# Long GpSimd operations in pieces of 256 columns, and three projections in the first token tile, in a two-layer hybrid decoder step

## The chip, the cores and the metric

The kernel runs on one core of a Trainium2 chip. Its engines have queues of their own: PE is TensorE (matrix products), DVE is VectorE (called Vector here), ACT is ScalarE, POOL is GpSimd (called Pool), SP issues DMAs. The metric is the time of one execution on the device in microseconds, the median of the runs.

## The reference

Two layers of a hybrid decoder over 1024 prompt tokens and 8 x 4 sampled tokens, 1056 in all, with a model width of 1024:

```python
def rms_norm(x, g):
    y = xf * lax.rsqrt(jnp.mean(xf * xf, axis=-1, keepdims=True) + EPS)
    return y * g
...
# each layer
#   x = x + W_out [ SWA-GQA-sink-attn(u) | Mamba2-SSD(u) ],  with u = RMSNorm(x)
#   x = x + SwiGLU(RMSNorm(x))
# W_in gives columns [q 512 | k 128 | v 128 | z 1024 | xBC 1536 | dt 16]
```

The columns xBC pass a causal convolution of four taps and a SiLU; they are 8 blocks of 128 columns of x (two heads of 64 each), two blocks of B and two of C. The SSD part scans 16 heads in chunks of 128 tokens with decays that come from dt; its output is gated by z and normed. The attention part has 8 query heads, 2 key heads, a window of 128 and a sink.

## The kernel before, in words

**Layout and products.** The activations lie with the model width on the partitions and the tokens along the columns. The tokens are cut into three token tiles of 352 columns (`TW`). Every projection is made in fp32r as three products of high and low halves: high x high (L293), high weight x low activation (L294), low weight x high activation (L295), over 8 blocks of 128 rows (k), so 24 products a token tile and 72 a block of 128 output columns. The projection `d` (dt, 16 columns) has two products a k (L289), 16 a tile. The low half of an activation (`alo`) is made by Vector or Pool (`split`, L248, and in the first norm L487) after ACT has made the high half (`ahi`).

**Weights.** `load_next` fetches the next weight by DMA on SP (L278), ACT makes its high half (L266), Pool its low half in one operation (L267). A weight is asked for one projection ahead (`AHEAD = 1`). Of the weights, 52 of W_in and 16 of the SSD rows of W_out have 8 k-blocks (1024 columns), 16 of the attention rows of W_out have 4 (512).

**Order.** The program is written once; a scheduler and the object `flow` decide the order on each engine. `proj(...)` makes one or several projections together, token tile by token tile, and calls `flow.tick()` after each tile and projection; side work pushed into `flow` (generators such as `steps`, `prep`, `both(j)`, which runs `ssd(j)`) goes a step on at a tick.

**The opening of a layer.** `d`, conv 10 (C of the first group, x10) and then conv 8 (B, x8) are projected. `steps` works out dt and the cumulated decays from `d`. Then come x0 to x7, z0 to z7 (the gates, L860, L864), v, q and k. In layer 0 a special piece of code makes the first norm from rows: squares on ACT (L473), transposes on PE (L467), products and casts by k.

**An SSD head pair (`ssd(j)`)**, twice for 512 tokens each: decays arrive by DMA in `bc`, ACT makes exponentials (L739, L740), Pool multiplies them by C (L741), Vector multiplies with the mask (L742); Vector's L732 makes x times dt or decay for PE's L748, which makes the states, and PE's L778 makes the outputs. Vector's L309 to L311 are the steps of a reciprocal root, L655 copies the convolution's three old columns, L1271 adds W_out's product to x.

## Time and profile before

| What | Value |
|---|---|
| Median of 3 runs | 2900.59 us (2896.8 to 2905.93) |
| The profiled execution's own time | 2900.49 us |
| Its span, first to last instruction | 2898.6 us |
| Mean granted clock of PE | 0.985 |
| PE busy | 2825.6 us (97%) |
| Vector busy | 1642.5 us (57%) |
| ACT busy | 1114.6 us (38%) |
| Pool busy | 983.5 us (34%) |

Busy times come from one profiled execution. A granted clock of 1.00 is 2.4 GHz, 0.5 is 1.2 GHz. The line numbers are those of the kernel before; an idle time in brackets on a row is that of the engine just before it, with the operation that ended it.

### The profile page before, as it was taken

How to read it: one execution, taken by the hardware profiler on the slowest of the kernel's cores; microseconds unless marked ns; L12 is line 12 of the kernel's file. 1: busy time of each engine (PE TensorE's matmuls, PEld its weight loads, DVE VectorE, ACT ScalarE, POOL GpSimd, SP SyncE). 2: the span in 40 equal slices, each digit the busy share in tenths (PEclk: the TensorE clock that was granted, in tenths of full speed). 3: DMA queues.
4: the chain of work that ended last, by engine and by line, in shares of the span. 5: the costliest groups of instructions: out<-in, count | busy, mean ns of one | idle time of the engine just before them, and what ended most of it. 6: DMA issues, size and time to landing. Idle time of an engine off the chain costs nothing. (4 is left out here: it accounts for less than half of the span.)

```text
span 2898.6 us, 46682 instructions
## 1 busy us (share of the span) xinstructions
PE 2825.6 (97%) x18456; PEld 2725.1 (94%) x18456; DVE 1642.5 (57%) x3639; ACT 1114.6 (38%) x2326; POOL 983.5 (34%) x884
## 2 busy tenths in 40 slices
PE   7999999999999999999988999999999999999999
PEld 6989898889999999999988898988899999999999
DVE  7765648756348862333487565587553678523232
ACT  5775737644212111111247666476431121112121
POOL 4343337435222222222243333365442222222221
PEclk8999999999999999999999999999999999999999
DMA  4222222102123321211222212220021333111112
GB/s 170 90 83 66 73 67 98 33 17 72 39 61 106 96 87 37 59 34 55 75 90 73 86 46 90 63 99 19 26 73 34 88 92 117 56 48 45 52 37 82
DMA packets 308323, 197.78 MB, mean 68 GB/s; under 512 B 28255, under 2 KB 287623, under 8 KB 308073
## 3 DMA queue, kind: packets, MB, share of 16 engines
q1 hardware_dynamic: 308072, 194.79, 22.4%
q8 instruction: 146, 2.39, 0.3%
q14 instruction: 73, 0.59, 0.1%
q10 hardware_dynamic: 32, 0.01, 0.0%
HBM read 171.49 MB, written 25.30 MB: 68 GB/s over the span
## 5 line engine op out<-in xcount | busy, mean ns | idle before, releaser
L293 PE MATMUL g<-ahi,whi 128*128 128x352 f32 x3744 | 1229.2, 329 | 6.6 <-DVE big L1271 5.8
L295 PE MATMUL g<-ahi,w 128*128 128x352 f32 x3744 | 1219.3, 326 | 0.0
L294 PE MATMUL g<-alo,whi 128*128 128x352 f32 x3744 | 1217.9, 325 | 0.0
L267 POOL TENSOR_TENSOR w<-w,whi 128x1024 fp32r<-128x1024 f32 (+2 forms) x248 | 512.4, 2066 | 1207.6 <-ACT whi L266 954.1
L293 PEld LDWEIGHTS g<-ahi,whi 128*128 128x128 f32 x3744 | 710.9, 190 | 21.5 <-issue 12.0
L294 PEld LDWEIGHTS g<-alo,whi 128*128 128x128 f32 x3744 | 713.5, 191 | 8.1 <-issue 4.1
L295 PEld LDWEIGHTS g<-ahi,w 128*128 128x128 f32 x3744 | 713.0, 190 | 4.8 <-issue 4.1
L266 ACT CAST whi<-w 128x1024 fp32r<-128x1024 f32 (+2 forms) x248 | 225.4, 909 | 663.6 <-PE g L294 636.3
L295 PE MATMUL g<-A,w 128*128 128x352 f32 x1104 | 357.2, 324 | 0.0
L293 PE MATMUL g<-A,whi 128*128 128x352 f32 x1104 | 356.8, 324 | 0.0
L294 PE MATMUL g<-F,whi 128*128 128x352 f32 x960 | 310.0, 323 | 0.0
L373 DVE TENSOR_TENSOR big<-g,big 128x352 f32<-128x352 f32 x240 | 125.4, 522 | 235.7 <-PE g L295 235.4
L295 PEld LDWEIGHTS g<-A,w 128*128 128x128 f32 x1104 | 208.1, 188 | 0.0
L293 PEld LDWEIGHTS g<-A,whi 128*128 128x128 f32 x1104 | 207.7, 188 | 0.0
L1350 DVE SCALAR_TENSOR_TENSOR F<-F,xdds 128x128 f32<-128x128 f32 x512 | 201.6, 419 | 9.6
L1335 DVE TENSOR_TENSOR R<-R,g 128x352 f32<-128x352 f32 x132 | 68.9, 522 | 218.4 <-PE g L295 217.1
L294 PEld LDWEIGHTS g<-F,whi 128*128 128x128 f32 x960 | 181.0, 189 | 0.0
L1332 ACT ACTIVATE R<-R 128x352 f32<-128x352 f32 x132 | 65.6, 497 | 297.3 <-DVE R L1331 297.0
L244 ACT CAST A<-R 128x352 fp32r<-128x352 f32 x132 | 64.1, 486 | 282.2 <-DVE R L1335 281.0
L669 DVE SCALAR_TENSOR_TENSOR big<-R,vc,big 128x352 f32<-128x352 f32 (+2 forms) x240 | 138.2, 605 | 21.8 <-ACT big L667 21.0
L741 POOL TENSOR_TENSOR F<-F,A 128x1024 f32<-128x1024 f32 x32 | 83.5, 2610 | 111.7 <-ACT F L740 111.7
L1331 DVE TENSOR_TENSOR R<-g,sc 128x352 f32<-128x352 f32 x88 | 45.9, 521 | 125.6 <-PE g L295 122.9
(366 smaller groups left out, 3529.4 us busy)
## 6 DMA issues: line engine op xcount, KB each, us to landing
w<-in_w_gate_up_dram SPq DMA_DIRECT2D x88, 512.0 KB
w<-in_w_in_dram SPq DMA_DIRECT2D x44, 512.0 KB
F<-acd SPq DMA_DIRECT2D x32, 512.0 KB
out_dram<-F SPq DMA_DIRECT2D x42, 256.0 KB
w<-in_w_down_dram SPq DMA_DIRECT2D x32, 320.0 KB
w<-in_w_down_dram SPq DMA_DIRECT2D x40, 256.0 KB
xd<-big SPq DMA_DIRECT2D x16, 528.0 KB
big<-xd SPq DMA_DIRECT2D x16, 528.0 KB
```

Source lines behind the costliest of these rows:

```text
L244: SC.copy(hi, src)
L266: SC.copy(hi, raw)
L267: G.tensor_tensor(lo, raw, hi.bitcast(F32), op=ALU.subtract)
L293: TE.matmul(out, lhsT=hi[:, k, c], rhs=xh, start=(start and k == 0), stop=False)
L294: TE.matmul(out, lhsT=hi[:, k, c], rhs=xl, start=False, stop=False)
L295: TE.matmul(out, lhsT=lo[:, k, c], rhs=xh, start=False, stop=(stop and k == nk - 1))
L373: flow.anchor = V.tensor_tensor(d, pt[:, 0:TW], d, op=ALU.add)
L669: flow.anchor = V.scalar_tensor_tensor(d, r(w), c_w(l, w, m), d, op0=ALU.mult, op1=ALU.add)
L741: G.tensor_tensor(bc, bc, ct[:, sl].unsqueeze(1).to_broadcast([P, 2, 512]), op=ALU.mult)
L1332: SC.activation(sg[t], sg[t], AF.Silu)
L1335: flow.anchor = V.tensor_tensor(sg[t], sg[t], pt[:, 0:TW], op=ALU.mult)
L1350: V.scalar_tensor_tensor(st[:, jj, :], bb[:, t, :], xdds[:, j, b * 4 + t:b * 4 + t + 1], st[:, jj, :], op0=ALU.mult, op1=ALU.add)
```

## The change

It has three parts. Pool's low halves of W_in and W_out weights are made in operations of two k-blocks (256 columns), those of gate, up and down as before. Pool's product of C and decays (128x1024) is made in four operations of 256 columns. And conv 8 is projected together with `d` and conv 10 in one `proj`, so that a token tile has 16 + 24 + 24 products, with `steps` pushed after it; the first norm of layer 0 becomes a plain loop over the token tiles, in which the squares of a tile stand ahead of its transposes, and Pool makes the low halves of six of the eight k in every tile (in tile 0 before: four).

```diff
--- before.py
+++ after.py
@@ -264,7 +264,10 @@
         hi = mk("whi", [P, nk, cw], F32R, bufs=3)
         lo = mk("w", [P, nk, cw], F32R, bufs=WB)
         SC.copy(hi, raw)
-        G.tensor_tensor(lo, raw, hi.bitcast(F32), op=ALU.subtract)
+
+        n = nk if k[1] in ("gu", "down") else 2
+        for a in range(0, nk, n):
+            G.tensor_tensor(lo[:, a:a + n], raw[:, a:a + n], hi[:, a:a + n].bitcast(F32), op=ALU.subtract)
         wready[k] = hi, lo
 
     def weights(key):
@@ -456,48 +459,29 @@
     u = act_tiles()
     rb = slot("F2", [P, T])
 
-    sizes = [[P if b < 8 else NS for b in range(3 * t, 3 * t + 3)] for t in range(NT)]
-
-    def blocks(t):
-        return slice(3 * t * P, 3 * t * P + sum(sizes[t]))
-
-    def rows_to_columns(t, src):
-        pt = pbank()
-        for i, m in enumerate(sizes[t]):
-            TE.transpose(pt[:, i * P:i * P + m], src(i)[0:m], ident[0:m, 0:m])
-        return pt[:, 0:sum(sizes[t])]
-
-    def roots(t):
-        for i, m in enumerate(sizes[t]):
+    for t in range(NT):
+        bs = range(3 * t, 3 * t + 3)
+        n = [P if b < 8 else NS for b in bs]
+        c0, w = 3 * t * P, sum(n)
+        for b, m in zip(bs, n):
             sq = slot("F1", [P, D])
-            SC.activation(sq[0:m], xr[3 * t + i][0:m], AF.Square, accum_out=s9[0:m, 3 * t + i:3 * t + i + 1])
-        return rsqrt("r3", s9[:, 3 * t:3 * t + 3], D, bufs=2)
-
-    def columns(t):
+            SC.activation(sq[0:m], xr[b][0:m], AF.Square, accum_out=s9[0:m, b:b + 1])
+
+        def rows_to_columns(src):
+            pt = pbank()
+            for i, m in enumerate(n):
+                TE.transpose(pt[:, i * P:i * P + m], src(i)[0:m], ident[0:m, 0:m])
+            return pt[:, 0:w]
+
         for k in range(KD):
-            pt = rows_to_columns(t, lambda i: xr[3 * t + i][:, k * P:(k + 1) * P])
-            (SC.copy if k % 2 and t else V.tensor_copy)(x[k][:, blocks(t)], pt)
-
-    def first_norm(t, y):
-        SC.copy(rb[:, blocks(t)], rows_to_columns(t, lambda i: y[:, i:i + 1].to_broadcast([P, P])))
+            pt = rows_to_columns(lambda i: xr[3 * t + i][:, k * P:(k + 1) * P])
+            (SC.copy if k % 2 and t else V.tensor_copy)(x[k][:, c0:c0 + w], pt)
+        y = rsqrt("r3", s9[:, 3 * t:3 * t + 3], D, bufs=1)
+        SC.copy(rb[:, c0:c0 + w], rows_to_columns(lambda i: y[:, i:i + 1].to_broadcast([P, P])))
         for k in range(KD):
             s = mk("nu", [P, TW], bufs=3)
             V.scalar_tensor_tensor(s, x[k][:, tsl(t)], g_mix(0, k), rb[:, tsl(t)], op0=ALU.mult, op1=ALU.mult)
-            hi = SC.copy(u[0][t][:, k, :], s)
-            (V if k % 4 == 3 or (k % 2 and t == 0) else G).tensor_tensor(u[1][t][:, k, :], s, u[0][t][:, k, :].bitcast(F32), op=ALU.subtract)
-        return hi
-
-    y = roots(0)
-    columns(0)
-    y1 = roots(1)
-    hi = first_norm(0, y)
-    columns(1)
-
-    with tc.issue_after(hi.ins):
-        y2 = roots(2)
-    first_norm(1, y1)
-    columns(2)
-    first_norm(2, y2)
+            split(u[0][t][:, k, :], u[1][t][:, k, :], s, V if k % 4 == 3 else G)
     vrow = slot("F1", [P, P])
     wrow = slot("F1", [P, P])
     SY.dma_start(out=cst[:, P:], in_=A["const"][:, P:])
@@ -738,7 +722,9 @@
                         SC.activation(tt[:, hh, c * P:(c + 1) * P], bc[:, hh, c * P:(c + 1) * P], AF.Relu, bias=acum[:, cc:cc + 1], scale=-1.0)
                 SC.activation(tt, tt, AF.Exp, scale=-1.0)
                 SC.activation(bc, bc, AF.Exp)
-                G.tensor_tensor(bc, bc, ct[:, sl].unsqueeze(1).to_broadcast([P, 2, 512]), op=ALU.mult)
+                for hh in range(2):
+                    for q in range(0, 512, 256):
+                        G.tensor_tensor(bc[:, hh, q:q + 256], bc[:, hh, q:q + 256], ct[:, hf * 512 + q:hf * 512 + q + 256], op=ALU.mult)
                 V.tensor_tensor(tt, tt, cm[:, hf * 4:hf * 4 + 4, :].rearrange("p c q -> p (c q)").unsqueeze(1).to_broadcast([P, 2, 512]), op=ALU.mult)
                 yield
             for hf in range(2):
@@ -896,9 +882,8 @@
         ct = slot("A0", [P, T])
         bt = mk("big", [P, T], bufs=8)
         proj(("d", 16, lambda t, pt: V.tensor_scalar(dtT[:, tsl(t)], pt[0:32, 0:TW], h16[:, l:l + 1], None, op0=ALU.add)),
-             conv(10, ct))
+             conv(10, ct), conv(8, bt))
         flow.push("steps", steps())
-        proj(conv(8, bt))
         flow.push("prep0", prep(0, ct, bt), 2)
         xs(0)
         xs(1)
```

**Where it moves instructions.** On PE, at the start of layer 1, in token tile 0, the products of `d` (`g_14184`) and of x10 (`g_14202`) alternated over the k before:

```order
L289 MATMUL g_14184<-alo_13572,whi_13808 16x352
L294 MATMUL g_14202<-alo_13572,whi_14174 128x352
L295 MATMUL g_14202<-ahi_13569,w_14175 128x352
L289 MATMUL g_14184<-ahi_13569,whi_13808 32x352
L293 MATMUL g_14202<-ahi_13569,whi_14174 128x352
L289 MATMUL g_14184<-alo_13572,whi_13808 16x352
L289 MATMUL g_14184<-ahi_13569,whi_13808 32x352
```

After it `g_14357` is `d`, `g_14375` is x10 and `g_14428` is x8 (lines L292, L296, L297, L298 are 289, 293, 294, 295 of before):

```order
L292 MATMUL g_14357<-alo_13730,whi_13966 16x352
L297 MATMUL g_14375<-alo_13730,whi_14332 128x352
L298 MATMUL g_14375<-ahi_13727,w_14333 128x352
L292 MATMUL g_14357<-ahi_13727,whi_13966 32x352
L296 MATMUL g_14375<-ahi_13727,whi_14332 128x352
L298 MATMUL g_14428<-ahi_13727,w_14342 128x352
L296 MATMUL g_14428<-ahi_13727,whi_14341 128x352
L297 MATMUL g_14428<-alo_13730,whi_14341 128x352
L298 MATMUL g_14428<-ahi_13727,w_14342 128x352
L296 MATMUL g_14428<-ahi_13727,whi_14341 128x352
L297 MATMUL g_14428<-alo_13730,whi_14341 128x352
L298 MATMUL g_14428<-ahi_13727,w_14342 128x352
```

Eleven products of x8 in a row (seven of them shown) now stand ahead of the next low product of `d`; in the kernel before all of x8 in this place came behind x10's tiles.

On Pool, at the start of layer 1, the low halves of the weights of x10 and x8 (`w_`) and of the first token tile's activations (`alo_`) stood so before:

```order
L267 TENSOR_TENSOR w_14175<-w_14172,whi_14174 128x1024
L248 TENSOR_TENSOR alo_13572<-nu_13976,ahi_13569 128x352
L248 TENSOR_TENSOR alo_13572<-nu_13980,ahi_13569 128x352
L248 TENSOR_TENSOR alo_13572<-nu_13984,ahi_13569 128x352
L267 TENSOR_TENSOR w_14181<-w_14178,whi_14180 128x1024
L248 TENSOR_TENSOR alo_13572<-nu_13992,ahi_13569 128x352
```

And after the change (L270 is the low half, now of 256 columns; `R_` is a convolution's buffer):

```order
L270 TENSOR_TENSOR w_14333<-w_14330,whi_14332 128x256 x4
L637 MEMSET R_14453 128x3
L248 TENSOR_TENSOR alo_13730<-nu_14134,ahi_13727 128x352
L248 TENSOR_TENSOR alo_13730<-nu_14138,ahi_13727 128x352
L248 TENSOR_TENSOR alo_13730<-nu_14142,ahi_13727 128x352
L270 TENSOR_TENSOR w_14342<-w_14339,whi_14341 128x256 x4
L248 TENSOR_TENSOR alo_13730<-nu_14150,ahi_13727 128x352
```

Each weight's row has become four operations, and the order between the weights and the activations' low halves stayed.

On ACT, at the start of layer 0, the squares (L473) of row blocks 6 to 8 (`F_22`, `F_23`) stood behind the casts of the first token tile (`ahi_117`) before:

```order
L486 CAST ahi_117<-nu_231 128x352
L486 CAST ahi_117<-nu_235 128x352
L486 CAST ahi_117<-nu_239 128x352
L473 ACTIVATE F_69_283,s_81<-F_22_111 128x1024
L473 ACTIVATE F_70_285,s_81<-F_23_113 128x1024
L473 ACTIVATE F_71_287,s_81<-F_24_115 32x1024
```

After it they are L468 (with `F_22`, `F_23`, `F_24`) and stand among copies of transposed rows (L478, L480) and the casts, which are now made by `split` (L244):

```order
L480 COPY F_31_126<-p_188 128x384
L468 ACTIVATE F_78_323,s_81<-F_22_114 128x1024
L478 COPY big_68<-p_236 128x384
L244 CAST ahi_120<-nu_193 128x352
L468 ACTIVATE F_79_325,s_81<-F_23_116 128x1024
L244 CAST ahi_120<-nu_197 128x352
L468 ACTIVATE F_80_327,s_81<-F_24_118 32x1024
```

The first of the three squares now stands ahead of the first cast, the second ahead of the second and the third behind it.

On PE, counted in products of projections, the four head pairs j = 0 to 3 of each layer stand 48 products later than before (the first L748 of layer 0 after 408 products instead of 360), j = 4 stands 24 later, and those from j = 5 where they stood.

## Rows read from the trace of the kernel before

**Rows 1.** Page, part 1: busy us, share of span, instructions of each engine.
```profile
PE 2825.6 (97%) x18456; PEld 2725.1 (94%) x18456; DVE 1642.5 (57%) x3639; ACT 1114.6 (38%) x2326; POOL 983.5 (34%) x884
```

**Rows 2.** Stretches: from, to, length, busy us of each engine, clock, DMA.
```profile
21.00:60.00 39.00, 32.70 (x149) 25.14 (x147) 32.83 (x69) 19.97 (x43) 17.44 (x18) 0.77 0.44 155
60.00:81.30 21.30, 21.30 (x133) 19.37 (x133) 14.28 (x31) 10.35 (x17) 9.66 (x12) 0.92 0.21 73
520.00:1450.00 930.00, 930.00 (x5802) 912.36 (x5801) 479.01 (x1013) 239.58 (x513) 279.51 (x252) 1.00 0.20 59
1459.20:1506.10 46.90, 39.90 (x241) 34.54 (x240) 38.75 (x86) 21.73 (x43) 27.28 (x24) 0.93 0.23 71
```

**Rows 3.** What PE waited for: total us, times, longest.
```profile
PE p L748 <- DVE F L732: 14.9, 6, 4.5
PE g L293 <- DVE big L1271: 5.8, 2, 2.9
```

**Rows 4.** Timeline, 211 to 216 us: start, duration, engine, line, operation, idle.
```profile
212.05 2.35 POOL L267 TENSOR_TENSOR w<-w,whi 128x1024 fp32r<-128x1024 f32 x1
...
212.26 2.48 DVE L864 TENSOR_TENSOR big<-big,nu 128x320 f32<-128x320 f32 x1 [2.41 <-ACT nu L860]
...
215.37 0.67 DVE L732 TENSOR_TENSOR F<-p,dt 128x512 f32<-128x512 f32 x1
...
215.50 0.71 PE L748 MATMUL p<-F,A 128*128 128x128 f32 x4 [4.46 <-DVE F L732]
```

**Rows 5.** Vector's instructions by line and shape: busy us, mean ns, idle.
```profile
L864 DVE TENSOR_TENSOR big<-big,nu 128x352 f32<-128x352 f32 x32 | 20.8, 655 | 51.1 <-ACT nu L860 51.1
```

**Rows 6.** Timeline of 494 to 503 us (Pool's operation in a row is x4).
```profile
494.47 4.01 POOL L248 TENSOR_TENSOR alo<-big,ahi 128x352 fp32r<-128x352 f32 x4
...
495.67 0.99 DVE L310 SCALAR_TENSOR_TENSOR F<-F 128x192 f32<-128x192 f32 x1
...
498.87 2.46 POOL L267 TENSOR_TENSOR w<-w,whi 128x1024 fp32r<-128x1024 f32 x1
...
499.17 2.38 DVE L310 SCALAR_TENSOR_TENSOR F<-F 128x192 f32<-128x192 f32 x1
...
501.47 0.51 DVE L1271 TENSOR_TENSOR big<-g,big 128x352 f32<-128x352 f32 x1
...
502.04 0.43 PE L293 MATMUL g<-ahi,whi 128*128 128x352 f32 x1 [2.91 <-DVE big L1271]
```

**Rows 7.** Timeline, 113 to 118 us.
```profile
113.96 2.44 POOL L741 TENSOR_TENSOR F<-F,A 128x1024 f32<-128x1024 f32 x1 [9.49 <-ACT F L740]
...
114.25 2.21 DVE L655 COPY R<-R 128x3 f32<-128x3 f32 x1
...
117.07 1.27 PE L748 MATMUL p<-F,A 128*128 128x128 f32 x5 [3.00 <-DVE F L732]
```

**Rows 8.** Timeline of Vector and PE: last low half, 192nd product.
```profile
65.21 0.53 DVE L487 TENSOR_TENSOR alo<-nu,ahi 128x352 fp32r<-128x352 f32 x1 [0.55 <-ACT ahi L486]
...
80.96 0.32 PE L295 MATMUL g<-ahi,w 128*128 128x352 f32 x1
```

**Rows 9.** Timeline of ACT: first of three squares, row blocks 6 to 8.
```profile
29.38 1.05 ACT L473 ACTIVATE F<-F 128x1024 f32<-128x1024 f32 x1
```

**Rows 10.** Timeline of Pool and PE, layer 1: last low halves, 192nd product.
```profile
1493.07 2.17 POOL L248 TENSOR_TENSOR alo<-nu,ahi 128x352 fp32r<-128x352 f32 x2 [1.47 <-ACT ahi L244]
...
1505.91 0.32 PE L295 MATMUL g<-ahi,w 128*128 128x352 f32 x1
```

**Rows 11.** Pool's instructions by line and shape: busy us, mean ns, idle.
```profile
L267 POOL TENSOR_TENSOR w<-w,whi 128x1024 fp32r<-128x1024 f32 x160 | 389.6, 2435 | 780.2 <-ACT whi L266 613.5 <-issue 165.0 <-POOL rc L665 0.8
...
L267 POOL TENSOR_TENSOR w<-w,whi 128x512 fp32r<-128x512 f32 x56 | 72.4, 1293 | 242.1 <-ACT whi L266 190.6 <-issue 51.5
```

**Rows 12.** Timeline of Pool and PE: C times decays, its reader.
```profile
176.08 6.38 POOL L741 TENSOR_TENSOR F<-F,A 128x1024 f32<-128x1024 f32 x2 [0.79 <-ACT F L740]
...
190.05 1.20 PE L778 MATMUL p<-F,A 128*64 128x128 f32 x18
```

## The prediction

> **What bounds the kernel now.** I read the page's list of busy times first. TensorE (PE) is busy 97% of the span [rows 1], so nothing is won by making another engine do less; only the time in which PE waits, or runs at its lower clock, can go. The reader should see 2898.6 - 2825.6 = 73 us of waiting in [rows 1], which is the whole stock together with the stretches at the lower clock. Next I cut the span into stretches. From 520 to 1450 us PE is busy 930.00 of 930.00 us at a granted clock of 1.00 [rows 2]: nothing to win there, and 930 / 5802 = 0.160 us is the price of one PE instruction at full clock. The start of layer 0 is the opposite: between 21 and 60 us PE does 149 instructions, which at 0.160 would be 23.8 us, in 39.0 us at a clock of 0.77; from 60 to 81.3 it is busy all the time. The start of layer 1, 1459.2 to 1506.1, is busy 39.90 of 46.90 us [rows 2].
>
> The list of waits then names what PE waited for [rows 3]. Hardly any of it names Pool: it names Vector operations. So I looked on the timeline at what held Vector. At 212 us Vector's product `big<-big,nu` (L864) lasts 2.48 us, beside a low half on Pool (L267, 2.35 us) that began 0.21 us earlier and ends 0.34 us before it; PE's L748 then waits 4.46 us for Vector's next operations, L732 [rows 4]. The same L864, one tenth wider, takes 655 ns on average elsewhere [rows 5], so it stood still for some 1.8 us of Pool's operation. At 499 us L310 takes 2.38 us beside a low half of 2.46 us, and PE waits 2.91 us for the L1271 behind it; the same operation took 0.99 us at 495.67, between short Pool operations [rows 6]. At 114 us a copy of three columns (L655) takes 2.21 us beside Pool's C times decays (L741, 2.44 us), and PE waits 3.00 us [rows 7]. These Vector operations read or write SBUF only; they and a running Pool operation exclude each other. L748 at 1645 us and L293 behind L1271 at 1932 us wait in the same way behind the same pairs of layer 1; the totals 14.9 and 5.8 us in [rows 3] contain them.
>
> **The change, part by part.** *1. Three products in the first token tile, and the rewritten first norm, layer 0.* The work stays the same: d, x10 and x8 are 16 + 24 + 24 products a tile. What moves is x8's 72. In the kernel before, 133 PE instructions are left to do after 60 us, at 0.160 each, and the last of the three groups' products begins at 80.96 us, although the last low half of the norm is done at 65.21 + 0.53 = 65.74 us [rows 8]. With x8 joined, the 48 products of its tiles 0 and 1 can go into the 39.0 - 23.8 = 15.2 us in which PE waited or ran slow: 48 x 0.160 = 7.7 us. With all 72 it is 11.5. I take the middle, -9.5. The bounds: -15 if that stretch were filled entirely; -3 if the three squares (1.05 us each, [rows 9]) that now stand between ACT's casts put the whole chain of the norm off by 3.15 us and the low clock stays, so that 48 products cost twice 0.160 while they fill waits (7.7 - 3.15, less a share for the clock). Pool also makes six instead of four of the first tile's eight low halves: two operations of 1.0 us (four L248, of the same size, in 4.01 us, [rows 6]) instead of two of 0.53 on Vector [rows 8], 0.9 us, inside these bounds. Nine small matmuls of `steps` go behind the 192 products; they keep their price.
>
> *2. The same in layer 1.* There 241 instructions x 0.160 = 38.6 us fill 46.9, so 8.3 us are free [rows 2]. The last low half lands at 1493.07 + 2.17 = 1495.24, and the last product begins 10.7 us later, at 1505.91 [rows 10]. The 48 products of x8's tiles 0 and 1 would be 7.7 us again, but they have only the idle 46.9 - 39.9 = 7.0 us to go into, and a part of it stands at the front, where nothing of x8 is ready either. I take -5, between 0 and -8.3.
>
> *3. Pieces.* The 68 input and ssm output weights of 1024 columns become four pieces, the 16 of 512 two, C times decays (32 times) four; gate, up and down stay. From the means 2435 ns for 1024 columns and 1293 for 512 [rows 11], a column costs 2.23 ns and an operation 0.15 us besides, so a piece takes 0.15 + 256 x 2.23 ns = 0.72 us and four take 2.89 instead of 2.44. A Vector operation that meets Pool then stands behind at most one piece, and keeps its turn if Vector gets in between two Pool operations. [Rows 6] show that it does: four Pool operations in a row take 4.01 us from 494.47, and L310 begins and ends within them. At each of the five places only one held Vector operation stands ahead of the ones PE needs (L864, L310, L655); L732 and L1271 behind them read PSUM and ran at 0.67 and 0.51 us. So each wait shrinks by 2.44 - 0.72 = 1.7 us: 5 x 1.7 = -8.5. The bounds: 0 if the pieces merely follow one another, and -20.7 if all of the waits 14.9 + 5.8 of [rows 3] vanish.
>
> *4. What the pieces cost.* Pool's own work grows by (68 + 32) x 0.45 + 16 x 0.15 = 47 us, spread over the two stretches that hold the attention and SSD parts. Pool is busy 34% [rows 1], and the list of PE's waits has none for L267 or L741; the cover is that a weight's low half is made one product ahead, 3 x 24 x 0.160 = 11.5 us, and that C times decays at 176.08 to 182.46 is read by PE only at 190.05 [rows 12], 7.6 us later. If that cover were gone, each weight would be 0.45 us late at least. Besides this, the heads' work of j = 0 to 3 comes later on PE (in layer 0 the first L748 after 408 products instead of 360, as the order has it), so that waits fall elsewhere. Bounds: 0 and +15 (three or four new waits like the 4.46); I take +3.5, less than one such wait, since the places themselves stay of one kind.
>
> **The sum.** -9.5 - 5 - 8.5 + 3.5 = -19.5 from the profiled execution's 2900.49 us gives **2881 us**. The median of the three runs shown is 2900.59, the same, so nothing is corrected. All bounds together would give 2900.49 - 44 = 2856 and 2900.49 + 12 = 2912 (-3, 0, 0, +15); they won't all fall on one side, so I use 2864 to 2900.
>
> **A rule that speaks against the pieces.** In [rows 4, 6, 7] the operation that began first, on Pool, ran at its usual speed and Vector's stood still. The Trainium skill, page "SBUF — State Buffer", section "Who interferes with whom", says that Vector and GpSimd share one pair of ports as an exclusive lock, which whoever issues first holds for the whole instruction while the other is blocked. By that rule a weight in four pieces has to win the lock four times, and a Vector operation may come in between each time; the page gives no price for it, and by it alone four pieces could take four Vector operations longer; rival D is this case, worked out from rows alone. The trace agrees with the rule as far as it holds Vector up; [rows 6] show both sides taking turns.
>
> **The rivals.**
> *A. Layer starts gain nothing.* The norm's own chain on ACT, Vector and Pool sets the end, and x8's products put PE's transposes off, which feed the chain. For it: Vector is busy 32.83 of 39.0 us there, as much as PE [rows 2]. Against it: after 65.74 us there was no norm left, and PE still had 15 us to do. It would give 2900.49 - 8.5 + 3.5 = 2895.5, within the 0.3% that a measurement of this kernel can tell from no change (8.7 us: 2891.9 to 2909.3).
>
> *B. Slower: the heads run into new waits.* With three products ahead of them, `steps` and the first four heads of each layer begin 48 products (7.7 us) later against the gates z that read them. Each head that comes too late costs a wait such as L748's 4.46 us [rows 4]. It decides when the new waits exceed the 19.5 + 3.5 = 23 us of gain, five such waits, and is slower by the measure at seven: eight, one a head in both layers, give 8 x 4.46 = 36 and 2900.49 - 23 + 36 = 2913. For it: PE's order changes there for about a thousand products of each layer. Against: the order of each head stays as it was, and heads from j = 5 stand where they stood.
>
> *C. Pieces don't let Vector in.* If four pieces run without a gap, Vector waits 2.89 us instead of 2.44 at each place: 5 x 0.45 = +2 instead of -8.5. Against it [rows 6]. It would give 2900.49 - 14.5 + 3.5 + 2 = 2891.5, on the edge of no change.
>
> *D. Pool starves.* If each piece waits for a Vector operation of 0.7 us (L864, [rows 5]), a low half takes 2.89 + 4 x 0.7 = 5.7 us. That is still under the 11.5 us of one projection, so PE waits only where two weights and C times decays come together. With the whole +15 of part 4 it would give 2900.49 - 23 + 15 = 2892.5, just within no change.
>
> **Chances.** The forecast and its neighbourhood below 2891.9: 0.66. A: 0.13; B: 0.08; C: 0.07, half of it on each side of the edge; D in a form that eats the gain: 0.06, most of it within 0.3%. Faster by over 0.3%: 0.66 + 0.04 + 0.02 = 0.72. Within: 0.13 + 0.03 + 0.02 = 0.18. Slower: 0.08 + 0.02 = 0.10. The range 2864 to 2900 leaves out B, a bad D, and a little of A and of the gains over 36 us: about 2 in 10.
>
> **What would show it.** Step 1 is right if the last of the 192 products of d, x10 and x8 ends near 71 us instead of 81.3, and step 2 if it ends near 1501 less what step 1 saved. Step 3 is right if Pool's pieces take about 0.72 us, L864 of 320 columns falls from 2.48 us to 1.4 or less (0.66 + 0.72), and the waits for L732 and L1271 at the five places are 1 to 3 us. The prediction is wrong if new waits of PE for L732, L742 or for the gates appear between 100 and 500 us or 1530 and 1930 us, or if PE's stretch from 21 to 60 us is as slow as before with the x8 products still behind it.

## The result and the profile after

The changed kernel takes 2866.4 us (median of four runs, 2858.3 to 2873.8) against 2903.26 before: a ratio of 0.9874, with a 95% interval of 0.984 to 0.9908, so 27 to 46 us less. A second measurement (below, with the experiments) gave 2859.83 against 2904.59, a ratio of 0.9842 (0.9829 to 0.9856). Both say faster. The forecast of 2881 was 15 to 21 us too high: the first median lies 2.4 us inside its range of 2864 to 2900, the second 4.2 us below it.

The profiled execution took 42.1 us less than that of before (span 2856.5 against 2898.6). The page's head and its list of busy times:

```profile
span 2856.5 us, 47073 instructions
...
PE 2809.2 (98%) x18456; PEld 2710.3 (95%) x18456; DVE 1623.0 (57%) x3637; ACT 1097.8 (38%) x2314; POOL 1050.1 (37%) x1202
```

PE's idle time, span less busy, is 2856.5 - 2809.2 = 47.3 us; it was 73.0 [rows 1]. So 25.7 us come from waits that are gone, and 16.4 from matmuls that ran faster, since their number is the same (x18456): more of them at the higher clock (the mean granted clock is 0.993, against 0.985).

The first stretches of [rows 2] at the same times, and 520 to 1400 us, since layer 1 begins earlier now (from, to, length, then busy time and instructions of PE, weight loads, Vector, ACT and Pool, then the granted clock):

```profile
21.00:60.00 39.00, 36.38 (x217) 29.10 (x216) 38.55 (x79) 22.12 (x47) 24.12 (x28) 0.96 0.46 156
60.00:81.30 21.30, 21.30 (x133) 20.97 (x132) 16.22 (x46) 12.25 (x23) 9.97 (x18) 0.92 0.30 98
520.00:1400.00 880.00, 880.00 (x5488) 864.02 (x5487) 446.60 (x939) 220.23 (x463) 268.12 (x248) 1.00 0.20 58
```

Between 21 and 60 us PE now does 217 instructions instead of 149, at a clock of 0.96 instead of 0.77. From 520 to 1400 us it is busy without a gap, as before.

The list of PE's waits:

```profile
PE p L823 <- ACT sc L819: 7.6, 4, 2.8
...
PE g L296 <- DVE big L1256: 5.8, 2, 2.9
```

The wait of L748 for L732, 14.9 us in six times in [rows 3], has no row any more (its lines are now L734 and L716). The wait behind the output projection's sum, L1271 then and L1256 now, is 5.8 us as it was. In front stands one that grew, for a copy of ACT's (L819, L833 before) in the work on the sampled tokens' states: 7.6 us, where it was 2.7.

The last of the 192 products of d, x10 and x8, in layer 0 and in layer 1, on PE's timeline of the changed kernel (both answer to [rows 8] and [rows 10]):

```profile
65.87 0.32 PE L298 MATMUL g<-ahi,w 128*128 128x352 f32 x1
```

```profile
1479.99 0.32 PE L298 MATMUL g<-ahi,w 128*128 128x352 f32 x1
```

In layer 0 it begins at 65.87 us instead of 80.96, 15.1 us earlier. In layer 1 the first of the 192 begins at 1437.65 (1459.28 before), so the stretch takes 42.3 us instead of 46.6.

Pool's and Vector's groups by line and shape (busy us, mean ns of one), and last Vector's L864 of 320 columns in the kernel before:

```profile
L270 POOL TENSOR_TENSOR w<-w,whi 128x256 fp32r<-128x256 f32 x304 | 237.6, 811 | 261.4 <-ACT whi L266 169.7 <-issue 90.0 <-POOL rc L649 0.8
L270 POOL TENSOR_TENSOR w<-w,whi 128x1024 fp32r<-128x1024 f32 x92 | 221.2, 2404 | 525.2 <-ACT whi L266 437.2 <-issue 87.1 <-POOL R L1298 0.7
L727 POOL TENSOR_TENSOR F<-F,A 128x256 f32<-128x256 f32 x128 | 109.4, 886 | 84.4 <-ACT F L724 84.4
```

```profile
L728 DVE TENSOR_TENSOR F<-F,A 128x1024 f32<-128x1024 f32 x32 | 55.6, 1738 | 60.9 <-ACT F L723 60.9
...
L850 DVE TENSOR_TENSOR big<-big,nu 128x320 f32<-128x320 f32 x16 | 14.8, 922 | 22.0 <-ACT nu L846 22.0
```

```profile
L864 DVE TENSOR_TENSOR big<-big,nu 128x320 f32<-128x320 f32 x16 | 34.5, 2159 | 28.1 <-ACT nu L860 28.1
```

A piece of 256 columns takes 0.81 us for the weights and 0.89 for C times decays, where I had 0.72. Vector's L864 of 320 columns (L850 now) has a mean of 0.92 us instead of 2.16; at 212 us it had taken 2.48 [rows 4].

### The profile page after: what moved, and what is told of

It reads as the page before. It is cut to its first block, busy times and chain, and to the rows that moved or that the text cites. A ratio compares the mean times of both kernels' runs of the same rounds, so it can differ in the third digit from the quotient of the medians.

```text
span 2856.5 us, 47073 instructions
## 1 busy us (share of the span) xinstructions
PE 2809.2 (98%) x18456; PEld 2710.3 (95%) x18456; DVE 1623.0 (57%) x3637; ACT 1097.8 (38%) x2314; POOL 1050.1 (37%) x1202
## 5 line engine op out<-in xcount | busy, mean ns | idle before, releaser
L296 PE MATMUL g<-ahi,whi 128*128 128x352 f32 x3744 | 1224.3, 327 | 7.2 <-DVE big L1256 5.8
L298 PE MATMUL g<-ahi,w 128*128 128x352 f32 x3744 | 1215.4, 325 | 0.0
L297 PE MATMUL g<-alo,whi 128*128 128x352 f32 x3744 | 1212.4, 324 | 0.0
L270 POOL TENSOR_TENSOR w<-w,whi 128x256 fp32r<-128x256 f32 (+3 forms) x468 | 560.8, 1217 | 1180.0 <-ACT whi L266 913.3
L296 PEld LDWEIGHTS g<-ahi,whi 128*128 128x128 f32 x3744 | 706.5, 189 | 18.9 <-issue 8.8
L297 PEld LDWEIGHTS g<-alo,whi 128*128 128x128 f32 x3744 | 709.2, 189 | 9.9 <-issue 7.4
L298 PEld LDWEIGHTS g<-ahi,w 128*128 128x128 f32 x3744 | 709.3, 189 | 9.1 <-issue 8.1
L298 PE MATMUL g<-A,w 128*128 128x352 f32 x1104 | 357.2, 324 | 0.0
L296 PE MATMUL g<-A,whi 128*128 128x352 f32 x1104 | 356.7, 324 | 0.0
L297 PE MATMUL g<-F,whi 128*128 128x352 f32 x960 | 310.0, 323 | 0.0
L298 PEld LDWEIGHTS g<-A,w 128*128 128x128 f32 x1104 | 208.1, 188 | 0.0
L296 PEld LDWEIGHTS g<-A,whi 128*128 128x128 f32 x1104 | 207.7, 188 | 0.0
L297 PEld LDWEIGHTS g<-F,whi 128*128 128x128 f32 x960 | 181.1, 189 | 0.0
L244 ACT CAST A<-R 128x352 fp32r<-128x352 f32 x132 | 64.1, 485 | 282.2 <-DVE R L1320 281.0
L727 POOL TENSOR_TENSOR F<-F,A 128x256 f32<-128x256 f32 x128 | 109.4, 886 | 84.4 <-ACT F L724 84.4
L1316 DVE TENSOR_TENSOR R<-g,sc 128x352 f32<-128x352 f32 x88 | 45.9, 522 | 125.4 <-PE g L298 122.9
```

The costliest lines, as they stand in the source:

```text
L244: SC.copy(hi, src)
L270: G.tensor_tensor(lo[:, a:a + n], raw[:, a:a + n], hi[:, a:a + n].bitcast(F32), op=ALU.subtract)
L296: TE.matmul(out, lhsT=hi[:, k, c], rhs=xh, start=(start and k == 0), stop=False)
L297: TE.matmul(out, lhsT=hi[:, k, c], rhs=xl, start=False, stop=False)
L298: TE.matmul(out, lhsT=lo[:, k, c], rhs=xh, start=False, stop=(stop and k == nk - 1))
L727: G.tensor_tensor(bc[:, hh, q:q + 256], bc[:, hh, q:q + 256], ct[:, hf * 512 + q:hf * 512 + q + 256], op=ALU.mult)
```

## The experiments

The change was cut into its halves, the order (three products, first norm) and the pieces, then these into theirs; then the pieces' length was changed. All times of a table row are its median, the ratio to the kernel before that ran beside it, and span, PE's busy time and their difference from its profiled execution.

| Kernel | us | Ratio (95%) | Span | PE busy | Idle |
|---|---|---|---|---|---|
| before | 2903 | 1 | 2898.6 | 2825.6 | 73.0 |
| e1 weights in pieces | 2883.05 | 0.9934 (0.9919 to 0.9949) | 2881.4 | 2821.0 | 60.4 |
| e2 C times decays in pieces | 2894.43 | 0.9973 (0.9962 to 0.9984) | 2891.3 | 2824.3 | 67.0 |
| e3 three products | 2880.46 | 0.9925 (0.9911 to 0.9939) | 2877.7 | 2818.7 | 59.0 |
| e4 first norm | 2892.24 | 0.9963 (0.9949 to 0.9978) | 2891.1 | 2819.2 | 71.9 |
| e5 three products and norm | 2876.16 | 0.9913 (0.9894 to 0.9932) | 2873.2 | 2812.0 | 61.2 |
| e6 both kinds of pieces | 2881.72 | 0.9929 (0.9909 to 0.9949) | 2881.7 | 2822.2 | 59.5 |
| changed kernel | 2866.4 | 0.9874 (0.984 to 0.9908) | 2856.5 | 2809.2 | 47.3 |
| e9 changed kernel again | 2859.83 | 0.9842 (0.9829 to 0.9856) | 2858.9 | 2810.6 | 48.3 |
| e7 pieces of 512 | 2858.13 | 0.9851 (0.983 to 0.9872) | 2855.7 | 2806.8 | 48.9 |
| e8 pieces of 128 | 2851.35 | 0.9826 (0.9805 to 0.9847) | 2852.6 | 2802.9 | 49.7 |
| e11 pieces of 64 | 2855.66 | 0.9836 (0.982 to 0.9851) | 2850.3 | 2801.0 | 49.3 |
| e10 gate, up, down too | 2856.71 | 0.9838 (0.9821 to 0.9855) | 2863.7 | 2815.1 | 48.6 |
| e12 C times decays whole | 2856.3 | 0.9835 (0.9821 to 0.9848) | 2859.0 | 2815.0 | 44.0 |

The column to read is the last. The two profiles of the changed kernel differ by 1.0 us in it, and it falls into steps: 73 before, 59 to 61 with one half of the change (e5, e6) or with its larger part alone (e1, e3), 44 to 50 with both. The smaller parts alone, e2 and e4, have 67 and 72.

**e1, only the weights in pieces.**

```diff
-        G.tensor_tensor(lo, raw, hi.bitcast(F32), op=ALU.subtract)
+        n = nk if k[1] in ("gu", "down") else 2
+        for a in range(0, nk, n):
+            G.tensor_tensor(lo[:, a:a + n], raw[:, a:a + n], hi[:, a:a + n].bitcast(F32), op=ALU.subtract)
```

> Only the low halves of the W_in and W_out weights in pieces. If the pieces take away PE's waits behind Pool: L748's waits at 215 and 1645 us fall from 4.4 to 2.7 us or less, the one at 117 us (C times decays) stays at 3.0, the layer starts stay as they are, and the time falls by 4 to 9 us. If instead the waits for L732 went away in the changed kernel because the heads stand 48 products later there: these waits stay above 3.5 us and the time stays within 3 us of before.

The waits for L732 fell from 14.9 to 8.6 us in total, none over 2.8, and the time by 19 us (0.9934). The pieces' theory held in direction, and the gain is twice its upper figure: idle time fell by 12.6 us, not only at the two places. Two waits, at 210 and 1631 us now, shrank to 2.83 us, a little more than the 2.7 expected. One expectation failed: the wait at 117 us (114 now), which was to stay at 3.0, was 1.29 us, though the copy of three columns took 2.24 us there beside the whole C times decays, as before. The layer starts stayed (the 192nd product 1.5 us earlier).

**e2, only C times decays in pieces.**

```diff
-                G.tensor_tensor(bc, bc, ct[:, sl].unsqueeze(1).to_broadcast([P, 2, 512]), op=ALU.mult)
+                for hh in range(2):
+                    for q in range(0, 512, 256):
+                        G.tensor_tensor(bc[:, hh, q:q + 256], bc[:, hh, q:q + 256], ct[:, hf * 512 + q:hf * 512 + q + 256], op=ALU.mult)
```

> Only C times decays in pieces. By the pieces' theory the wait at 117 us falls from 3.0 to 1.3 us and those at 215 and 1645 us stay at 4.4; 1 to 4 us less. By the theory of the moved heads nothing changes beyond 2 us. Either way Pool's pieces of 256 columns take some 0.85 us on average, as in the changed kernel.

7.8 us less by the ratio, more than either theory had. The waits went otherwise than both expected. The one at 117 us (114 now) fell to 2.03, and those at 215 and 1645 us (211 and 1638 now), which were to stay at 4.4 because the weights' low halves are whole here, fell to 2.58 and 2.56. PE's waits for L732, and Vector and Pool ahead of the first of the two:

```profile
PE p L750 <- DVE F L732: 8.8, 5, 2.6
```

```profile
209.89 0.60 DVE L866 TENSOR_TENSOR big<-big,nu 128x320 f32<-128x320 f32 x1 [2.41 <-ACT nu L862]
...
210.10 2.61 POOL L267 TENSOR_TENSOR w<-w,whi 128x1024 fp32r<-128x1024 f32 x1
```

L866 is L864 there. It began 0.21 us ahead of the whole low half, beside the last of C times decays' four pieces, and took 0.60 us; in [rows 4] it began 0.21 us behind the low half and took 2.48. So such a wait also hangs on a few tenths of a microsecond in the order of arrival, and a piece in one operation can free a place that was put down to another.

The profile of e2 also shows how far chance goes: up to product 300 this kernel's instructions on PE are those of the kernel before in the same order, and yet its 192nd product came 4.5 us earlier. The stretch from 31 to 60 us in the kernel before and in e2 (the clock is the third number from the end):

```profile
31.00:60.00 29.00, 26.43 (x113) 20.30 (x113) 22.86 (x49) 14.39 (x31) 11.77 (x14) 0.71 0.47 176
```

```profile
31.00:60.00 29.00, 26.31 (x138) 20.05 (x138) 23.46 (x48) 14.54 (x31) 14.56 (x18) 0.89 0.47 177
```

0.71 against 0.89: the same order of work at another clock, 113 instructions against 138 in nearly the same busy time. A difference of some 4 us at the start of one profiled execution therefore shows nothing by itself.

**e3, only the three products in the first token tile.**

```diff
-             conv(10, ct))
+             conv(10, ct), conv(8, bt))
         flow.push("steps", steps())
-        proj(conv(8, bt))
```

> Only x8 joined to d and x10 in one projection; first norm and Pool's operations as before. If x8's products fill the waits of the first token tiles: the last of the 192 products begins near 66 to 70 us instead of 80.96, some 3 us are won at the start of layer 1, together 13 to 18 us. If the rewritten first norm is what sets the start of layer 0: it begins at 78 us or later, and no more than 4 us are won. If the moved heads took away the waits for L732, these are below 2 us in total here and the time falls by 5 us or more beyond that; by the pieces' theory there are 8 us of them or more, at other places perhaps.

The 192nd product began at 67.48 us, as the first theory had it. The time fell by 22 us, a little more than its 18, and idle time by 14; the start of layer 1 took 43.5 us instead of 46.6. The moved heads did both things that were in dispute. PE's waits in e3:

```profile
PE p L837 <- ACT sc L833: 12.8, 4, 6.4
PE g L293 <- DVE big L1270: 5.8, 2, 2.9
...
PE p L748 <- DVE F L732: 2.8, 2, 1.4
```

L748's waits for L732 are nearly gone without any piece, 2.8 us instead of 14.9, though not below the 2 that I had asked for; in their place stand 12.8 us for L833 (2.7 before). So the theory of the moved heads was right about L748, and the rival of new waits was right that others come, at a price that takes about as much.

**e4, only the plain first norm.**

```diff
-    y = roots(0)
-    columns(0)
-    y1 = roots(1)
-    hi = first_norm(0, y)
...
+    for t in range(NT):
...
+            split(u[0][t][:, k, :], u[1][t][:, k, :], s, V if k % 4 == 3 else G)
```

> Only the first norm of layer 0 written as a plain loop. If x8's products make the gain: the last of the 192 products begins within 3 us of 80.96, and the time stays within 4 us of before. If the norm's rewriting makes it: that product begins near 70 us and 8 us or more are won.

Between the two: the 192nd product began at 74.71 us, 6.3 us earlier, and the time fell by 10.7 us by the ratio (6 to 15). Idle time is 71.9 against 73.0, so hardly any wait went; PE's stretch from 21 to 60 us ran at a clock of 0.82:

```profile
21.00:60.00 39.00, 35.35 (x180) 27.03 (x181) 35.12 (x74) 19.99 (x43) 25.63 (x27) 0.82 0.44 153
```

Its gain in the profile is thus nearly all clock (PE's busy time is 6.4 us less), but a clock of 0.82 lies within what the kernels with the old norm and order show there (0.77 before, 0.74 in e1, 0.91 in e2). The ratio is clear of no change; where the gain comes from is not shown. Together with the three products (e5 beside e3) it is worth 4 us by the medians, with intervals that overlap.

**e5 and e6, the two halves.**

> The changed kernel without its pieces: three products and the plain first norm. If pieces and order are separate gains: 15 to 17 us less at the 192nd product as in the changed kernel, no gain between there and the end of layer 0, 8 us in layer 1's heads as with three products alone, 24 to 27 us in all, and a wait of PE for L833's work on ACT of over 10 us. If the moved heads alone made the gain after the start: 33 us or more, as the changed kernel.

> Both kinds of pieces and nothing else. If the two kinds act at different places: 20 to 27 us less, waits for L732 below 5 us in total. If they share the same waits, so that the second finds nothing left: no more than 20 us less, as with the pieces of the weights alone. The 192nd product stays within 5 us of 80.96 us.

e5 gave 25.3 us less, with a wait of 11.7 us for L833's copy, as the theory of separate gains had it; in the profile 14.1 us of it are there at the 192nd product and 25.4 at the end, where the theory's 15 to 17 and nothing more in layer 0 were a little off. e6 gave 20.6 us, the two 45.9 together; the changed kernel has 36.6 in its first measurement and 45.9 in its second. In the profiled executions they add up to the microsecond: spans 25.4 and 16.9 us shorter, together 42.3, and the changed kernel 42.1. Idle time: 11.8 and 13.5, together 25.3, and 25.7. The halves are separate gains. In e6 the 192nd product begins at 74.81 us, 6.2 us earlier and so 1 us beyond the 5 that I had allowed; e2 shows 4.5 us of chance.

e6's waits of PE for the head work, and behind the output projection's sum:

```profile
PE p L753 <- DVE F L735: 6.9, 5, 2.6
PE g L296 <- DVE big L1276: 5.9, 2, 2.9
```

L753 and L735 are L748 and L732 there: 6.9 us, where below 5 was expected if the two kinds of pieces act at different places. With 20.6 us against e1's 19.2, C times decays adds nothing that can be measured.

What a piece does can be seen between e5 (whole operations) and the changed kernel at the same places of the program. The first is `steps` in layer 1; POOL, Vector and PE on the timeline of e5:

```profile
1504.75 3.06 POOL L267 TENSOR_TENSOR w<-w,whi 128x1024 fp32r<-128x1024 f32 x1 [1.38 <-ACT whi L266]
...
1505.62 2.29 DVE L575 TENSOR_SCALAR nsq<-nsq 128x160 f32<-128x160 f32 x1
...
1508.77 0.29 DVE L578 TENSOR_TENSOR nsq<-dt,bc 128x128 f32<-128x128 f32 x1
...
1509.12 0.79 PE L582 MATMUL p<-nsq,cst 128*128 128x128 f32 x2 [2.62 <-DVE nsq L578]
```

and of the changed kernel (L578, L581, L585 are e5's L575, L578, L582):

```profile
1496.68 4.27 POOL L270 TENSOR_TENSOR w<-w,whi 128x256 fp32r<-128x256 f32 x4
...
1499.58 0.77 DVE L578 TENSOR_SCALAR nsq<-nsq 128x160 f32<-128x160 f32 x1
...
1502.26 0.28 DVE L581 TENSOR_TENSOR nsq<-dt,bc 128x128 f32<-128x128 f32 x1
...
1502.59 0.49 PE L585 MATMUL p<-nsq,cst 128*128 128x128 f32 x2 [0.91 <-DVE nsq L581]
```

The same Vector instruction takes 2.29 us beside a whole low half and 0.77 beside four pieces, and PE's wait behind it falls from 2.62 to 0.91 us. The four pieces took 4.27 us here instead of 3.06, with Vector in between, and PE's list of waits has no row for them. The second is the copy of three columns (L655 before) beside C times decays, in e5 and in the changed kernel:

```profile
118.83 2.45 POOL L722 TENSOR_TENSOR F<-F,A 128x1024 f32<-128x1024 f32 x1 [12.51 <-ACT F L721]
...
119.12 2.22 DVE L636 COPY R<-R 128x3 f32<-128x3 f32 x1
```

```profile
115.10 2.20 POOL L727 TENSOR_TENSOR F<-F,A 128x256 f32<-128x256 f32 x3 [9.26 <-ACT F L724]
...
115.39 0.55 DVE L639 COPY R<-R 128x3 f32<-128x3 f32 x1
```

2.22 and 0.55 us. Two more waits that go between e5 and the changed kernel stand in one row of e5:

```profile
PE p L748 <- DVE F L723: 4.1, 2, 2.1
```

L723 is Vector's product with the mask. Ahead of the first of these waits it takes 3.27 us, from 213.24, beside a whole low half from 213.06 to 215.43; the row for L723's successor L728 is gone from the changed kernel's list. Not all of the 13.9 us of idle time between the two kernels can be told so: 4.1 us of it stand in the waits for ACT's copy (L814, L819 now; 11.7 against 7.6, and 8.9 in e9), and no held operation is shown for these.

**e7, e8 and e11, pieces of 512, 128 and 64 columns.** The `2` of the first loop became 4, 1, or 1 with two pieces a k-block, and the 256 of the second 512, 128 and 64.

> The changed kernel with pieces of 512 columns. A piece takes some 1.3 us. If the length that Vector may stand behind counts: 3 to 8 us slower than the changed kernel, between it and the one without pieces. If it only counts that Vector gets in at all, or that Pool's order is broken up: within 3 us of the changed kernel. If the pieces' own fixed cost counted, it would be faster than the changed kernel.

> The changed kernel with pieces of 128 columns. A piece takes 0.15 + 128 x 2.23 ns = 0.44 us alone, a weight's eight 3.5 us. If Vector's wait behind a piece counts: up to 4 us faster than the changed kernel. If the fixed cost and the turns with Vector count (Pool starved): slower by 3 us or more, with waits of PE or ACT for Pool's low halves in the list.

> The changed kernel with pieces of 64 columns: 0.15 + 64 x 2.23 ns = 0.29 us each by my line through the means, 4.7 us for a weight's sixteen. If shorter is better without end: as fast as pieces of 128 (2851 us) or faster. If the fixed cost of an operation starves Pool: slower than pieces of 128 by 5 us or more, with waits for L270 on ACT's or PE's side and Pool busy over 1250 us.

One of the theories of the length fell. Pieces of 512 are as fast as those of 256 (2858 and 2860 us, idle 48.9 and 48.3), although one takes 1.35 us; those of 64 also, although Pool's low halves take 16 x 0.361 = 5.8 us instead of 2.4 and Pool is busy 1274.5 us. Those of 128 have the lowest median, 2851 us; their interval overlaps the others', and idle time is no less. Pool's groups in e7, e8 and e11:

```profile
L270 POOL TENSOR_TENSOR w<-w,whi 128x512 fp32r<-128x512 f32 x192 | 256.9, 1352 | 471.1 <-ACT whi L266 343.4 <-issue 119.7 <-ACT R L646 7.1
```

```profile
L270 POOL TENSOR_TENSOR w<-w,whi 128x128 fp32r<-128x128 f32 x608 | 293.4, 515 | 222.3 <-ACT whi L266 133.6 <-issue 87.9 <-POOL R L1298 0.5
```

```profile
L273 POOL TENSOR_TENSOR w<-w,whi 128x64 fp32r<-128x64 f32 x1216 | 396.1, 361 | 151.9 <-issue 109.1 <-ACT whi L266 38.8 <-POOL xs L1139 1.6
```

The length does show in the waits, behind the output projection's sum, in e7, e8 and e11 (L1259 is L1256 there):

```profile
PE g L296 <- DVE big L1256: 7.6, 2, 3.8
```

```profile
PE g L296 <- DVE big L1256: 4.6, 2, 2.3
```

```profile
PE g L299 <- DVE big L1259: 1.8, 2, 0.9
```

With pieces of 256 it is 5.8. Added over all its rows, PE's waiting for Vector is 22.9 us in the changed kernel and 14.4 in e11, but its waiting for Pool rises from 3.8 to 8.0 us and that for ACT from 10.2 to 14.4. So at 64 columns Vector holds PE up less, and other waits take it back. Pool's order at these places differs too between the kernels, so the length's own share is not separated.

**e9, the changed kernel again.**

> The changed kernel once more, beside the kernel before, to size it against the pieces of other lengths. If its first runs (2858 to 2874 us) only differ by where the lower clock fell: a median of 2858 to 2866 us, near the sum of the two halves (-25.3 and -20.6 us, so 2857). If the two halves share a gain: 2863 to 2870 us.

2859.83 us, within the first alternative: the first four runs went with their mean clock (0.993 at 2858.3, 0.991 at 2866, 0.988 at 2873.8 us), and those of e9 lie between 2856 and 2862.

**e10, the low halves of gate, up and down in pieces too.**

> The changed kernel with the low halves of gate, up and down in pieces of 256 columns too. In the stretch of these weights PE is busy throughout in the kernel before, so if pieces only count where PE waits behind Vector: within 3 us of the changed kernel, Pool's busy time up by some 70 us. If pieces cost Pool or Vector time that comes to PE: slower by 4 us or more, with idle PE between 520 and 1420 us.

2856.71 us, no difference, as the first alternative had it, and Pool's busy time up by 76 us. The stretch of these weights in e10, to be set beside the third row of the changed kernel's stretches above:

```profile
520.00:1400.00 880.00, 880.00 (x5494) 863.94 (x5493) 398.98 (x944) 221.74 (x467) 305.71 (x432) 1.00 0.20 58
```

PE is busy 880.00 us of 880 in both; Vector's busy time is 398.98 us instead of 446.60, since it stands still less, and that is worth nothing here.

**e12, C times decays whole in the changed kernel.**

> The changed kernel with C times decays in one operation as before. If the two kinds of pieces share the same waits, as they seemed to in the old order: within 4 us of the changed kernel. If C times decays acts at places of its own: 5 to 10 us slower, with waits of PE for L732's successor behind L741.

2856.3 us, no slower, idle time 44.0. The operation is back at its length:

```profile
L725 POOL TENSOR_TENSOR F<-F,A 128x1024 f32<-128x1024 f32 x32 | 85.0, 2666 | 87.4 <-ACT F L724 87.4
```

So this part of the change brings nothing in the new order. The place at which it held up PE before [rows 7] is one that the moved heads have cleared: the copy of three columns takes 2.25 us again beside the whole operation, and PE's list of waits has no row for the products of x times dt or decay (L732 before), which waited behind the copy.

## Why the prediction was right, and where its sizes were off

**The bound** was read rightly: only waits and lower clock could go, and they went, 25.7 and 16.4 us.

**Step 1, the start of layer 0.** I took -9.5, between -3 and -15; the profile shows -15.1 (-13.8 in e9, where the product begins at 67.14 us). The mechanism is the one named: x8's products fill the stretch from 21 to 60 us, in which PE does 208 to 217 instructions with the three products joined (e3, e5, the changed kernel, e9) and 148 to 173 with the old order and norm (before, e1, e2, e6). The size is in part luck. PE's order is the same up to the 192nd product in before, e1, e2 and e6, and it began at 80.96, 79.42, 76.49 and 74.81 us; the profile that the forecast is measured against has the latest. In the nine profiles with the three products it began between 64.28 (e8) and 68.38 us (e12). Between the means, 77.9 and 66.4, lie 11.5 us, near the -9.5. I had left the clock to the bounds, and it rose from 0.77 to 0.96 (0.91 in e9); but e2 has 0.91 with the old order, so how much of the clock the change brings is not shown. The feared delay by the three squares did not show in the time; in e4, which has them alone, PE's waits for the first step of the norm's root (L305) were 7.8 us instead of 4.9, and the kernel was faster all the same.

**Step 2, the start of layer 1.** -5 forecast, 46.6 - 42.3 = -4.3 measured. That is not the order's doing alone: with the order and no pieces it is -3.1 (e3) and -1.9 (e5), so the term was about twice too large, and the rest came when the pieces joined it.

**Step 3, the pieces.** -8.5 forecast, with +3.5 for their cost; the pieces are worth 16.7 us in the profile (e5 against the changed kernel) and 16.9 (e6 against before); by the ratios it is 20.6 us in e6, and 11.3 and 20.6 from e5 to the changed kernel's two measurements. Of the three gains this is the one that was mis-sized most. The mechanism is shown, by the two pairs of rows above. The pricing failed in three ways. The five places were not the places: most of L748's waits went with the moved heads already (e3), and the waits behind L1271 did not shrink at all. There I had read that one held instruction stands ahead, which is so in the kernel before. In the changed kernel the low half begins earlier in Vector's string, and four stand beside it (the first, L314 from 477.76 us, is not shown). Its timeline:

```profile
477.73 3.29 POOL L270 TENSOR_TENSOR w<-w,whi 128x256 fp32r<-128x256 f32 x4
...
478.60 1.04 DVE L948 TENSOR_TENSOR A<-A,F 128x352 f32<-128x352 f32 x1
479.57 0.88 DVE L312 TENSOR_TENSOR F<-F 128x192 f32<-128x192 f32 x1
480.48 0.76 DVE L313 SCALAR_TENSOR_TENSOR F<-F 128x192 f32<-128x192 f32 x1
...
481.16 0.51 DVE L1256 TENSOR_TENSOR big<-g,big 128x352 f32<-128x352 f32 x1
...
481.73 0.43 PE L296 MATMUL g<-ahi,whi 128*128 128x352 f32 x1 [2.94 <-DVE big L1256]
```

Vector's operations with two inputs in SBUF take turns with the four pieces now and last 0.76 to 1.04 us each (L310, of L313's kind, took 0.99 so in [rows 6]), and the L1256 that PE wants comes after all of them, as late as it came after one long stall. What rival C described for all places, no gain since Vector waits as long in parts as in one, holds at this place with pieces of 256, and with those of 512 the wait is longer (3.8 us). The gain came from other places that I had not counted, of 1 to 2.6 us each, such as `steps` in layer 1 and Vector's product with the mask. And a wait costs more than its length: after the waits at 117 and 215 us the kernel before ran on at 1.2 GHz, which is a granted clock of 0.50, and the changed kernel, without a wait at the second place and with a shorter one at the first, did not:

```profile
117.30:120.70 3.40, 3.40 (x15) 3.40 (x15) 3.40 (x8) 3.39 (x9) 3.39 (x2) 0.50 0.00 0
216.30:219.70 3.40, 3.40 (x15) 3.40 (x14) 3.40 (x16) 0.13 (x2) 0.28 (x1) 0.50 0.00 0
```

```profile
116.00:119.40 3.40, 3.40 (x23) 2.77 (x23) 3.36 (x11) 3.40 (x6) 3.40 (x5) 1.00 0.00 0
213.00:216.40 3.40, 3.25 (x31) 2.56 (x31) 3.40 (x14) 1.68 (x3) 1.53 (x4) 1.00 0.02 7
```

I had the waits at their bare length. (After the unchanged wait of 2.94 us behind L1256 the changed kernel, too, ran at 0.50, from 483.1 to 486.4 us.) Last, the price of a stall as one piece's length (2.44 to 0.72 us) is not what the times follow, since 512 columns do as well as 64. That Vector gets its turn at all within a low half is what the times show to count; why the length counts for so little is settled only in part, by the other waits that rise with pieces of 64. The scheduler also orders 1 to 3% of PE's rows otherwise when the pieces' length changes, and no run kept the order fixed while it changed the length, so a part of the differences between e7, e8, e9 and e11, and of the pieces' gain itself, may be order; e2 shows a place where arrival by a few tenths decided.

**Step 4, the costs.** Pool's work grew by 1050.1 - 983.5 = 66.6 us instead of 47, with Vector's turns in it, and PE's waits for Pool did not grow, 3.8 us in all against 4.9. With 1274.5 us (e11) they were 8.0, without loss of time. Rival D's starving did not come with pieces of 256. The Trainium skill, page "SBUF — State Buffer", section "Who interferes with whom", whose rule of an exclusive lock spoke against the pieces, agrees with the trace in both directions: Vector's L575 lasted until 0.1 us after the end of a whole operation, and the pieces took 4.27 us with Vector in between. Vector's own long operation L742 (L728) pays too, with a mean of 1738 ns against 1381.

**The rivals.** A (no gain at the starts) is out by steps 1 and 2. B (new waits of the moved heads) was right that new waits come, 12.8 us for L833 in e3, but its count of one wait a head was wrong: the old ones went in exchange, and idle time in e3 fell by 14.0 us in all. In e5 the span beyond the two starts shrank by 25.4 - 14.1 - 1.9 = 9.4 us (the 192nd product began at 66.89, and layer 1's stretch took 44.7). I had put this on the side of the costs. The 42.1 us of the profiles are thus 14.1 and 1.9 at the two starts, 9.4 in the moved heads and 16.7 from the pieces, against -9.5, -5, +3.5 and -8.5: the two largest gains were priced too small, and what was wrong in the sum above all is the account of the moved heads, for which I priced new waits and not the old ones that go.

## What to carry to other kernels

Where GpSimd and VectorE share their operands' memory, cut GpSimd's long operations so that VectorE gets a turn within them; a cut in two already did for the time all that cuts in four to sixteen did here, and it only counts where TensorE waits behind VectorE. Price a wait of TensorE with the slow stretch that follows it, and ask of each stalled queue how many instructions stand ahead of the one that is wanted: where there were several, pieces of 256 columns only spread the stall. Such a collision hangs on a few tenths of a microsecond, so a wait that goes after a change isn't proof of what the change did there: look for the held operation. When independent products are at hand, put them where the first ones wait for their inputs; that was worth as much as all the pieces.

## What the runs showed of the hardware that was not expected

TensorE's instructions, in the same order, ran at a granted clock of 0.71 in one execution and 0.89 in another over 29 us, and the 192nd product came 4.5 us earlier in the second (before and e2). VectorE's busy time contains the time it stands still beside GpSimd: it fell from 1623.0 to 1523.9 us from the changed kernel to e10 with no change of the time. And GpSimd's subtraction took 361, 515, 811 and 1352 ns for 64, 128, 256 and 512 columns with VectorE's turns in it, so a piece costs more than the line through the longer ones (0.29 us for 64) says.
